# A transposition and a state product of the RWKV pairs issued in turn, on all four quarters of the array

## The chip, the cores and the metric

The kernel runs on one core of a Trainium2 chip. The metric is the device time of one execution in microseconds; of the kernel before there are three runs. A core has five engines that run side by side and wait for one another through semaphores: TensorE (PE in the profile; its weight loads are listed apart as PEld), VectorE (DVE), ScalarE (ACT), GpSimd (POOL), and SyncE (SP), which here issues most DMAs. Products land in PSUM, which ScalarE and VectorE empty.

TensorE is an array of 128 rows by 128 columns. A product whose two sizes are at most 64 needs only one quarter of it. Which quarter is settled by where the operands and the result lie: the rows by the partitions of the operands (0 to 63, or 64 to 127), the columns by the partitions of the result.

## The reference

A decoder trunk of two layers over 1024 tokens of width 1024, in float32. The first layer mixes with 8 retention heads and 8 RWKV-7 heads of width 64, the second with sliding-window attention; each layer has a SwiGLU block. The RWKV heads carry a state that every token updates:

```python
def step(state, inp):
    r_t, w_t, k_t, v_t, a_t, b_t = inp
    sa = jnp.einsum('bhij,bhj->bhi', state, a_t)
    state = state * w_t[:, :, None, :] + sa[..., None] * b_t[:, :, None, :] + v_t[..., None] * k_t[:, :, None, :]
    return state, jnp.einsum('bhij,bhj->bhi', state, r_t)
```

The kernel does this in chunks of 64 tokens. For each chunk it forms the products of the keys and decays among themselves, inverts a triangular matrix for the effect of each token on the later ones (the solve), and then steps the state once a chunk.

## The kernel before, in words

The first mixer (`mixer0`, L502) works on two halves of 512 tokens. Its work is written as Python generators, each with a letter: `a` the first norm; `b` to `e` the four units (two pairs of heads each: a half's pairs 0 and 1, or 2 and 3); `f` to `m` the eight pairs of RWKV heads (`pair`); `n` to `u` the eight retention heads' pairs (`ret`); `v` the second half's norm. `F` is the input projection, `W` the first half's output projection. The class `Plan` (L156) runs these generators against a virtual clock (`plan.now`) of estimated PE time and an account of PSUM banks in use (`plan.banks`), and so settles the order in which the program is emitted. The order of the products on PE is then fixed by hand: `PE_ORDER` (L105) lists entries such as `f11:16`, the next 16 products into the 12th PSUM tile (counted from 0) of stream f, or `f5,6:8`, eight products in turn from tiles 5 and 6. `pe_order` (L312) chains them. The orders on the other engines and the DMA queues are left to the framework, which schedules with a simulated timeline.

A pair works on two heads at once, head 0 in partitions 0 to 63 and head 1 in 64 to 127, over 8 chunks. The tiles of PSUM that matter here are all of the tag "m", of which there are four buffers (banks) for all streams together; `pst` (L390) hands them out in turn, and the next tile of a buffer waits until the one before has been read. A pair's tiles, in order: 0 and 1 the low-rank projections, 2 the norm, 3 the triangular matrix (DT) for the solve, 4 the bonus (bv, L869), 5 to 8 the matrices GG (read by VectorE, L885), 9 and 10 the transposition of BK (L891), and then:

- tile 11 (L894 to L899): the transposition of AR, as 16 products with the identity, head 0 on rows and columns 0 to 63, head 1 on rows and columns 64 to 127: the two diagonal quarters of the array. ScalarE copies the result to the first half of the tile XA.
- tiles 12 and 13: transpositions of v by 128 columns (L304), from which VectorE makes UV (L908 to L928).
- tile 14 (L934 to L939): 16 products of GG by UV. Here head 0's result comes from operands in partitions 64 to 127 and head 1's from 0 to 63: the other two quarters. ScalarE copies the result to the second half of XA.

The unit of the pair reads XA only after its solve (31 steps on VectorE, L966 and L970, a trip through DRAM, and products into tiles of tag "c"), for the products of GT by XA. In `PE_ORDER` tile 11 stands before the transpositions of v and tile 14 some microseconds later, with products of other streams between them. The retention stream emits into the same four banks: tiles 0 and 1 transposed k and v (L1174, L1176), 2 and 3 the scores (masked by VectorE, L1191), 4 the chunk states (L1213), 5 and 6 the outputs (6 is ps_m<-r,Sc), 7 the norm. `second_norm` (L663) loads the second half of x and squares it on ScalarE (L673); later its gained copies (L578, L579) become the second half's operand of F.

Of the kernel before, what the change touches and what calls it, by code (L numbers as in the profile page):

```python
# [10 lines left out]
F32 = mybir.dt.float32  # L11
# [5 lines left out]
P = 128  # L17
# [8 lines left out]
NCH = 8  # L26
# [77 lines left out]

PE_ORDER = """  # L105
F0:13 F1:2 F0:3 F1:14 F0:3 F1:3 F0:3 F1:3 F0:2 F1:2 F2:2 a0:1 F2:22 F3:24 f0:1 f1:1 F4:24 F5:24 F6:15 f2:1 F6:9
F7:24 g0:1 g1:1 F8:9 f3:16 F8:9 g2:1 F8:6 F9:18 f4:1 F9:6 F10:6 f5,6:8 f7,8:8 F10:17 f9:8 f10:8 f11:16 f12:4
g3:16 f13:4 n0:4 n1:4 g4:1 F10:1 F11:12 f14:16 g5:1 g6:2 g5:2 g6,5:3 g7:1 g8:2 g7:2 F11:12 F12:3 g8,7:3 g9:8
g10:8 F12:13 g11:16 g12:4 n2,3:8 g13:4 F12:8 F13:5 n4:8 n5:8 F13:16 n6:8 g14:16 F13:3 F14:21 n7:1 F14:3 F15:24
F16:6 o0:4 o1:4 F16:18 F17:3 o2,3:8 o4:8 F17:21 o5:1 o6:1 o5:7 b0:32 o6:7 h0:1 h1:1 F18:18 b1:32 o7:1 F18:6  # L110
F19:12 b2:8 h2:1 b3:8 b4:8 F19:12 b5:8 b6:16 b7:8 b8:8 F20:24 F21:13 b9:16 b10:8 h3:16 b11:8 b12:4 F21:8 i0:1
i1:1 b13:4 F21:3 F22:24 F23:6 b14:4 i2:1 F23:6 b20:1 b15:4 b20:15 b21:6 b16:4 b21:4 b22:16 b23:5 F23:9 b23:1
b21:2 b17:4 b23:6 h4:1 F23:3 F24:11 b21:1 b18:4 b21:1 b23:2 h5:4 b21:1 b19:4 b21:1 b23:2 F24:12 h6:4 b24:1 F24:1
F25:24 F26:7 b25:1 b26:1 h7:4 h8:4 b27:1 h9:8 F26:11 h10:8 h11:16 h12:4 i3:16 h13:4 p0:4 F26:6 F27:9 p1:4 i4:1
p2:2 p3:2 p2,3:4 h14:16 i5,6:4 i5:2 i6:2 i7:4 i8:4 F27:15 F28:2 p4:8 i9:8 i10:8 F28:6 i11:16 i12:4 p5:8 p6:8
i13:4 F28:16 F29:19 v0:1 p7:1 i14:16 F29:5 F30:7 q0:4 q1:4 F30:3 F31:2 F30:3 F31:11 q2,3:8 F30:9 F31:6 F30:2
F31:2 q4:8 q5:8 F31:3 F32:6 q6:8 F32:18 F33:22 q7:1 c0:32 F33:2 F34:23 c1:32 F34:1 F35:20 c2:8 c3:8 c4:8 j0:1
F35:4 F36:11 j1:1 c5:8 c6:16 c7:8 c8:8 j2:1 F36:9 c9:16 c10:8 c11:8 c12:2 F36:4 F37:10 c12:2 F37:14 F38:7 j3:5
c13:4 j3:11 k0:1 k1:1 F38:8 c20:5 c14:4 c20:11 c21:6 c22:1 c21:2 c15:4 c22:15 c23:4 c21:2 c23:1 c16:4 c23:5 k2:1
F38:9 F39:8 c17:4 c21:2 c23:2 j4:1 F39:16 F40:2 c21:1 c18:4 c21:1 c23:2 j5:4 c21:1 c19:4 c21:1 c23:2 F40:3 j6:4  # L120
F40:19 F41:12 c24:1 F41:12 F42:24 c25:1 c26:1 j7,8:8 c27:1 j9:8 F43:13 j10:8 j11:16 j12:4 k3:16 j13:4 k4:1
F43:11 F44:11 j14:16 k5,6:8 k7:4 k8:4 F44:9 k9:8 k10:8 k11:16 k12:4 r0:4 r1:4 F44:4 F45:10 k13:4 r2,3:8 r4:8
F45:12 k14:16 r5:8 r6:8 l0:1 l1:1 F45:2 F46:17 r7:1 l2:1 F46:7 F47:24 m0:1 m1:1 F48:24 F49:1 l3:1 F49:17 d0:1
l3:3 d0:31 l3:12 m2:1 d1:32 F49:6 F50:15 d2:8 d3,4:16 d5:8 F50:9 F51:2 d6:16 d7:8 m3:16 d8:8 d9:16 d10:8 d11:8
F51:8 s0,1:8 d12:4 F51:14 F52:2 d13:4 F52:19 s2:1 d14:4 s3,2:7 F52:3 F53:3 d15:4 s4:8 F53:18 s5:2 d16:4 s6:8
d20:3 s5:6 d17:4 d20:13 d21:13 d18:4 d21:1 d22:16 d23:3 d21:1 d19:4 d21:1 d23:13 l4:1 F53:3 F54:14 m4:1 s7:1
l5:3 l6:3 l5:1 l6:1 d24:1 F54:10 F55:17 d25:1 d26:1 F55:7 F56:9 l7:4 l8:4 d27:1 l9:8 l10:8 l11:16 l12:4 m5:3
m6:3 m5:1 m6:1 l13:4 F56:15 m7:2 m8:2 m7,8:4 m9:8 m10:8 t0:4 t1:4 F57:24 m11:16 m12:4 t2:4 e0:2 t3:4 l14:16
m13:4 t4:8 t5:8 t6:4 e0:4 m14:1 t6:4 m14:15 e0:26 F58:24 F59:15 t7:1 e1:32 u0:4 u1:4 F59:9 W0:7 e2:8 e3:8 e4:8
u2:4 W0:17 W1:11 u3:4 e5:8 u4:8 e6:16 e7:8 e8:8 u5:8 u6:8 e9:16 e10:8 e11:8 e12:2 u7:1 e20:5 e12:2 e20:11 e21:4  # L130
e22:6 e13:4 e22:10 e23:4 e21:2 e14:4 e23:2 W1:13 W2:14 e15:4 e21:1 W2:10 W3:13 e21:1 e23:2 e21:1 e16:4 e21:1
e23:2 W3:11 W4:9 e17:4 e21:2 e23:2 W4:15 W5:4 e21:1 e18:4 e21:1 e23:2 W5:20 e19:4 e21:2 W6:24 W7:3 e23:2 e24:1
e25:1 e26:1 e27:1 W7:21
"""


# [121 lines left out]
class Kern:  # L258
# [518 lines left out]
    def pair(self, u, hf, p):  # L777


        nc, mp = self.nc, self.mp  # L780
        V, S, G = nc.vector, nc.scalar, nc.gpsimd
        ident = self.cst["ident"]
        half = (slice(0, 64), slice(64, 128))
# [8 lines left out]
        ps = self.pst("m", [P, HT])  # L792
# [15 lines left out]
        ps = self.pst("m", [P, HT])  # L808
# [14 lines left out]
        AR = self.t(mp, [P, NCH, P], "AR", 4)  # L823
# [12 lines left out]
        ps = self.pst("m", [P, NCH, 64])  # L836
# [13 lines left out]
        for q in range(4):  # L850
            r0 = 32 * q
# [14 lines left out]
        ps = self.pst("m", [P, HT])  # L866
# [8 lines left out]
        for h in range(2):  # L875
            pss = [self.pst("m", [P, 4, P]) for _ in range(2)]
            for i in range(4):
                for e in range(2):
                    c = 4 * h + i
# [7 lines left out]
        for e in range(2):  # L887
            ps = self.pst("m", [P, NCH, 64])
            rs = half[e]
# [1 line left out]
                self.tr(ps[:, c, :], BK[rs, c, e : e + 2, :].rearrange("p a t -> p (a t)"), ident[rs, rs])  # L891
            S.copy(GG[:, :, e, P:], ps)
        yield (), 0.6
        XA = self.t(mp, [P, NCH, P], "XA", 2)  # L894
        ps = self.pst("m", [P, NCH, 64])
        for c in range(NCH):
            for rs in half:
                self.mm(ps[rs, c, :], AR[rs, c, 0:64], ident[rs, rs], start=True, stop=True)
        S.copy(XA[:, :, 0:64], ps)  # L899
        UV = self.t(mp, [P, NCH, 2, 64], "UV", 2)  # L900
        UVw = UV.rearrange("p (j two) e t -> p j two e t", two=2)
        for w in range(2):
            ps = self.pst("m", [P, 4, 2, 64])
# [27 lines left out]
                )  # L931
            yield (), 1.0
        yield (), 7.5
        ps = self.pst("m", [P, NCH, 64])  # L934
        for c in range(NCH):
            for e in range(2):
                b = half[1 - e]
                self.mm(ps[half[e], c, :], GG[b, c, e, 0:64], UV[b, c, e, :], start=True, stop=True)
        S.copy(XA[:, :, 64:P], ps)  # L939
        st.update(AR=AR, UV=UV, bv=bv, PC=PC, GG=GG, XA=XA)  # L940
        self.plan.done(f"a{u}_{p}")

    def unit(self, u, hf, pairs):
# [77 lines left out]
        for st, GT in zip(sts, GTs):  # L1021
            GG, XA, UV = st["GG"], st["XA"], st["UV"]
            for h in range(2):
                cc = slice(4 * h, 4 * h + 4)
                ps = self.pst("m", [P, 4, P])
                for i in range(4):
                    for a in half:
                        self.mm(ps[a, i, :], GT[a, 4 * h + i, :], XA[a, 4 * h + i, :], start=True, stop=True)
                for e, a in enumerate(half):
# [5 lines left out]
        for st in sts:  # L1035
            GG, XA, UV, AR = st["GG"], st["XA"], st["UV"], st["AR"]
            M, C0 = XA[:, :, 0:64], XA[:, :, 64:P]
# [1010 lines left out]
```

## Time and profile before

| | |
|---|---|
| median of three runs | 2292.93 us (2292.22 to 2293.02) |
| the profiled execution's own time | 2295.7 us |
| its span, first to last instruction | 2293.9 us |
| PE busy | 2261.0 us, 99% of the span, 13056 instructions |
| DVE, ACT, POOL busy | 74%, 46%, 44% |
| granted TensorE clock, mean | 0.997 |
| first mixer | about the first 660 us |

A row of the view in order of time gives the start in microseconds from the span's start, the length from the first start to the last end, the engine, the line, the operation, output tile and inputs, the shape, and how many instructions were merged; in brackets the idle time of the engine before it and who ended it. A row "64*64" used 64 rows and 64 columns of the array. A float32 product is two instructions (passes) on PE, so 16 products show as x32. The view of waits gives who waited for whom, the sum in microseconds, how often, and the longest. The view of one line or tile gives shortest, median and longest duration in ns, and first and last start.

### The profile page before, as it was taken

What the parts mean: (1) busy time and instruction counts of PE and PEld (TensorE: products, weight loads), DVE (VectorE), ACT (ScalarE), POOL (GpSimd) and SP (SyncE); (2) the same over time, 40 slices, a digit from 0 to 9 for tenths busy, and PEclk for the clock granted to TensorE, in tenths of its full rate; (3) what the DMA queues carried; (4) which work ended last, traced back from release to release, by engine and by line L of the source; (5) the groups of instructions that cost most, each with busy time, mean ns of one, the idle gap of its engine ahead of it and who ended that gap; (6) DMA issues with size and microseconds to landing.
All of it is one profiled execution on the core that took longest, in us unless ns stands there. A gap on an engine that the chain in (4) does not pass through costs nothing.

```text
span 2293.9 us, 35742 instructions
## 1 busy us (share of the span) xinstructions
PE 2261.0 (99%) x13056; PEld 1810.2 (79%) x13056; DVE 1698.6 (74%) x2635; ACT 1047.1 (46%) x1947; POOL 1006.5 (44%) x796
## 2 busy tenths in 40 slices
PE   8999999999999999999999999999999999999998
PEld 6777777778878888888888887787788888888886
DVE  6877855876567358888896967858748788888867
ACT  5454544424445333333343466656745333333335
POOL 3123221202341067777777501113203677778675
PEclk9999999999999999999999999999999999999999
DMA  7566644444446455556766332123246566557663
GB/s 271 194 214 207 195 150 136 140 116 125 144 182 219 164 179 211 211 202 220 261 224 245 108 120 71 52 92 124 85 140 226 171 215 215 210 202 279 226 225 115
DMA packets 170337, 406.43 MB, mean 177 GB/s; under 512 B 43185, under 2 KB 45873, under 8 KB 170161
## 3 DMA queue, kind: packets, MB, share of 16 engines
q1 hardware_dynamic: 166752, 397.59, 50.5%
q10 hardware_dynamic: 2832, 4.45, 0.5%
q8 instruction: 104, 1.70, 0.3%
q0 software_dynamic: 576, 2.10, 0.2%
q14 instruction: 73, 0.59, 0.1%
HBM read 275.48 MB, written 123.21 MB: 174 GB/s over the span
## 4 chain that ended last, share of the span: by engine, by line
PE 77%; DVE 10%; ACT 5%; DMA 3%; issue 3%; SPq 1%; POOL 1%; DVEq 0%; ACTq 0%; POOLq 0%
PE ps_f L293 9%; PE ps_m L1300 7%; PE ps_m L1303 7%; PE ps_m L1302 7%; PE ps_m L293 6%; PE ps_f L1300 5%; PE ps_f L1302 5%; PE ps_f L1303 5%; PE ps_f L450 2%; PE ps_f L447 2%; PE ps_f L449 2%; PE ps_r L1300 2%; PE ps_c L1303 2%; PE ps_r L1303 2%; PE ps_r L1302 2%
## 5 line engine op out<-in xcount | busy, mean ns | idle before, releaser
L293 PE MATMUL ps_f<-n,w 128*128 128x512 f32 x1440 | 360.8, 404 | 9.7 <-ACT w L432 5.8
L293 PEld LDWEIGHTS ps_f<-n,w 128*128 128x128 f32 x1440 | 268.4, 190 | 84.4 <-issue 14.1
L433 POOL TENSOR_TENSOR w<-wr,w 128x512 fp32r<-128x512 f32 x63 | 87.2, 1390 | 300.9 <-ACT w L432 293.3
L432 ACT CAST w<-wr 128x512 fp32r<-128x512 f32 x231 | 141.1, 617 | 160.2 <-PE ps_f L450 53.0
L433 DVE TENSOR_TENSOR w<-wr,w 128x512 fp32r<-128x512 f32 x168 | 117.6, 703 | 64.0 <-ACT w L432 63.5
L1300 PE MATMUL ps_f<-n,w 128*128 128x512 f32 x415 | 164.2, 396 | 0.0
L1302 PE MATMUL ps_f<-n,w 128*128 128x512 f32 x415 | 162.7, 392 | 0.0
L1303 PE MATMUL ps_f<-n,w 128*128 128x512 f32 x415 | 162.6, 392 | 0.0
L433 POOL TENSOR_TENSOR w<-wq,w 128x512 fp32r<-128x512 f32 x91 | 130.5, 1444 | 31.6 <-ACT w L432 31.6
L1300 PE MATMUL ps_m<-n,w 128*128 128x512 f32 x333 | 130.4, 392 | 0.0
L1302 PE MATMUL ps_m<-n,w 128*128 128x512 f32 x333 | 129.6, 389 | 0.0
L1303 PE MATMUL ps_m<-n,w 128*128 128x512 f32 x333 | 129.5, 389 | 0.0
L1310 DVE TENSOR_TENSOR nq<-ps_m,u 128x512 f32<-128x512 f32 x88 | 58.9, 684 | 92.2 <-PE ps_m L1303 92.2
L1730 POOL TENSOR_SCALAR s<-s,st 128x256 f32<-128x256 f32 (+1 forms) x32 | 30.6, 955 | 192.0 <-ACT w L432 61.3
L464 POOL TENSOR_TENSOR n<-nq,n 128x512 fp32r<-128x512 f32 x60 | 100.1, 1681 | 7.6 <-ACT n L462 7.6
L1495 POOL TENSOR_TENSOR w<-wd,w 128x512 fp32r<-128x512 f32 (+1 forms) x62 | 87.8, 1425 | 32.4 <-ACT w L1494 30.5
L1300 PEld LDWEIGHTS ps_f<-n,w 128*128 128x128 f32 x415 | 77.9, 188 | 20.2 <-issue 3.8
L1300 PE MATMUL ps_m<-cb,w 128*128 128x512 f32 x236 | 91.9, 389 | 0.4 <-DVE nq L1310 0.4
L1302 PEld LDWEIGHTS ps_f<-n,w 128*128 128x128 f32 x415 | 77.9, 188 | 17.7 <-issue 2.0
L1303 PE MATMUL ps_m<-cb,w 128*128 128x512 f32 x236 | 91.8, 389 | 0.0
L1302 PE MATMUL ps_m<-cb,w 128*128 128x512 f32 x236 | 91.8, 389 | 0.0
L1303 PEld LDWEIGHTS ps_f<-n,w 128*128 128x128 f32 x415 | 77.9, 188 | 16.8 <-issue 0.7
(521 smaller groups left out, 6494.1 us busy)
## 6 DMA issues: line engine op xcount, KB each, us to landing
hc<-n SPq DMA_DIRECT2D x84, 512.0 KB, 3.2
wsp<-w SPq DMA_DIRECT2D x54, 512.0 KB, 3.3
w<-wsp SPq DMA_DIRECT2D x54, 512.0 KB, 3.5
n<-hc SPq DMA_DIRECT2D x54, 512.0 KB, 6.2
wq<-in_w_gate SPq DMA_DIRECT2D x44, 512.0 KB, 4.5
u<-u SPq DMA_DIRECT2D x88, 256.0 KB, 2.9
ha<-hc SPq DMA_DIRECT2D x34, 512.0 KB, 5.6
hid<-n SPq DMA_DIRECT2D x66, 256.0 KB, 2.0
```

What stands on the lines that cost most here:

```text
L293: i = self.nc.tensor.matmul(out, lhsT, rhs, **kw)
L432: nc.scalar.copy(hi[:, :n], raw[:, c])
L433: self.lo.tensor_tensor(out=lo[:, :n], in0=raw[:, c], in1=hi.bitcast(F32)[:, :n], op=ALU.subtract)
L447: x = nc.tensor.matmul(ps, hi, rh, start=k == 0, stop=False)
L449: y = nc.tensor.matmul(ps, hi, rl, start=False, stop=False)
L450: z = nc.tensor.matmul(ps, lo, rh, start=False, stop=k == n - 1)
L464: e.tensor_tensor(out=lo, in0=src, in1=hi.bitcast(F32), op=ALU.subtract)
L1300: i = mm(ps, hi, xh, start=first and k == 0, stop=False, skip_group_check=True)
L1302: mm(ps, hi, xl, start=False, stop=False, skip_group_check=True)
L1303: mm(ps, lo, xh, start=False, stop=last and k == len(w) - 1, skip_group_check=True)
L1310: self.last_add = V.tensor_tensor(out=o, in0=x, in1=y, op=ALU.add)
L1495: nc.gpsimd.tensor_tensor(out=lo, in0=v, in1=hi.bitcast(F32), op=ALU.subtract)
```

## The change

Tile 11 goes from its place. Its 16 products are issued where those of tile 14 were, one of each in turn, so that successive products use the quarters (rows 0, columns 0), (rows 64, columns 0), (rows 64, columns 64), (rows 0, columns 64), and so on. The two copies to XA follow one another. The transpositions of v are now tiles 11 and 12, and the two groups are tiles 13 and 14, allocated one after the other. The planner's clock and its account of banks are advanced at the old place as if tile 11 were still there and put back at the new one, so that the emission order of all the rest is as before. In `PE_ORDER` each pair's 16 entries of tile 11 are taken out, and the 16 of tile 14 become 32 of both in turn at the same place; nothing else in it moves.

```diff
-        XA = self.t(mp, [P, NCH, P], "XA", 2)
-        ps = self.pst("m", [P, NCH, 64])
-        for c in range(NCH):
-            for rs in half:
-                self.mm(ps[rs, c, :], AR[rs, c, 0:64], ident[rs, rs], start=True, stop=True)
-        S.copy(XA[:, :, 0:64], ps)
+        self.plan.banks.append(self.plan.now + 3.0)
+        for _ in range(2 * NCH):
+            self.plan.now += max(0.05, 0.00167 * 64 * 0.6)
...
         yield (), 7.5
-        ps = self.pst("m", [P, NCH, 64])
+        XA = self.t(mp, [P, NCH, P], "XA", 2)
+        pa, ps = (self.pst("m", [P, NCH, 64]) for _ in range(2))
+        self.plan.banks.pop()
+        now = self.plan.now
+        for c in range(NCH):
+            for e in range(2):
+                b = half[1 - e]
+                self.mm(pa[half[e], c, :], AR[half[e], c, 0:64], ident[half[e], half[e]], start=True, stop=True)
+        self.plan.now = now
         for c in range(NCH):
             for e in range(2):
                 b = half[1 - e]
                 self.mm(ps[half[e], c, :], GG[b, c, e, 0:64], UV[b, c, e, :], start=True, stop=True)
+        S.copy(XA[:, :, 0:64], pa)
         S.copy(XA[:, :, 64:P], ps)
```

The entries of `PE_ORDER` for pair g, before and after; the other seven change in the same way:

```diff
-g10:8 F12:13 g11:16 g12:4 n2,3:8 g13:4 F12:8 F13:5 n4:8 n5:8 F13:16 n6:8 g14:16 F13:3
+g10:8 F12:13 g11:4 n2,3:8 g12:4 F12:8 F13:5 n4:8 n5:8 F13:16 n6:8 g13,14:32 F13:3
```

More of the change, by code (lines that the diff above doesn't have):

```diff
@@ L106 @@
 F0:13 F1:2 F0:3 F1:14 F0:3 F1:3 F0:3 F1:3 F0:2 F1:2 F2:2 a0:1 F2:22 F3:24 f0:1 f1:1 F4:24 F5:24 F6:15 f2:1 F6:9
[L107 to L130, printed above, removed]
@@ L131 @@
-e22:6 e13:4 e22:10 e23:4 e21:2 e14:4 e23:2 W1:13 W2:14 e15:4 e21:1 W2:10 W3:13 e21:1 e23:2 e21:1 e16:4 e21:1
-e23:2 W3:11 W4:9 e17:4 e21:2 e23:2 W4:15 W5:4 e21:1 e18:4 e21:1 e23:2 W5:20 e19:4 e21:2 W6:24 W7:3 e23:2 e24:1
-e25:1 e26:1 e27:1 W7:21
+F7:24 g0:1 g1:1 F8:9 f3:16 F8:9 g2:1 F8:6 F9:18 f4:1 F9:6 F10:6 f5,6:8 f7,8:8 F10:17 f9:8 f10:8 f11:4 g3:16
+f12:4 n0:4 n1:4 g4:1 F10:1 F11:12 f13,14:32 g5:1 g6:2 g5:2 g6,5:3 g7:1 g8:2 g7:2 F11:12 F12:3 g8,7:3 g9:8 g10:8
+F12:13 g11:4 n2,3:8 g12:4 F12:8 F13:5 n4:8 n5:8 F13:16 n6:8 g13,14:32 F13:3 F14:21 n7:1 F14:3 F15:24 F16:6 o0:4
@@ new lines @@
+o1:4 F16:18 F17:3 o2,3:8 o4:8 F17:21 o5:1 o6:1 o5:7 b0:32 o6:7 h0:1 h1:1 F18:18 b1:32 o7:1 F18:6 F19:12 b2:8
+h2:1 b3:8 b4:8 F19:12 b5:8 b6:16 b7:8 b8:8 F20:24 F21:13 b9:16 b10:8 h3:16 b11:8 b12:4 F21:8 i0:1 i1:1 b13:4
+F21:3 F22:24 F23:6 b14:4 i2:1 F23:6 b20:1 b15:4 b20:15 b21:6 b16:4 b21:4 b22:16 b23:5 F23:9 b23:1 b21:2 b17:4
+b23:6 h4:1 F23:3 F24:11 b21:1 b18:4 b21:1 b23:2 h5:4 b21:1 b19:4 b21:1 b23:2 F24:12 h6:4 b24:1 F24:1 F25:24
+F26:7 b25:1 b26:1 h7:4 h8:4 b27:1 h9:8 F26:11 h10:8 h11:4 i3:16 h12:4 p0:4 F26:6 F27:9 p1:4 i4:1 p2:2 p3:2
@@ new lines @@
+p2,3:4 h13,14:32 i5,6:4 i5:2 i6:2 i7:4 i8:4 F27:15 F28:2 p4:8 i9:8 i10:8 F28:6 i11:4 p5:8 p6:8 i12:4 F28:16
+F29:19 v0:1 p7:1 i13,14:32 F29:5 F30:7 q0:4 q1:4 F30:3 F31:2 F30:3 F31:11 q2,3:8 F30:9 F31:6 F30:2 F31:2 q4:8
+q5:8 F31:3 F32:6 q6:8 F32:18 F33:22 q7:1 c0:32 F33:2 F34:23 c1:32 F34:1 F35:20 c2:8 c3:8 c4:8 j0:1 F35:4 F36:11
+j1:1 c5:8 c6:16 c7:8 c8:8 j2:1 F36:9 c9:16 c10:8 c11:8 c12:2 F36:4 F37:10 c12:2 F37:14 F38:7 j3:5 c13:4 j3:11
+k0:1 k1:1 F38:8 c20:5 c14:4 c20:11 c21:6 c22:1 c21:2 c15:4 c22:15 c23:4 c21:2 c23:1 c16:4 c23:5 k2:1 F38:9 F39:8
@@ new lines @@
+c17:4 c21:2 c23:2 j4:1 F39:16 F40:2 c21:1 c18:4 c21:1 c23:2 j5:4 c21:1 c19:4 c21:1 c23:2 F40:3 j6:4 F40:19
+F41:12 c24:1 F41:12 F42:24 c25:1 c26:1 j7,8:8 c27:1 j9:8 F43:13 j10:8 j11:4 k3:16 j12:4 k4:1 F43:11 F44:11
+j13,14:32 k5,6:8 k7:4 k8:4 F44:9 k9:8 k10:8 k11:4 r0:4 r1:4 F44:4 F45:10 k12:4 r2,3:8 r4:8 F45:12 k13,14:32 r5:8
+r6:8 l0:1 l1:1 F45:2 F46:17 r7:1 l2:1 F46:7 F47:24 m0:1 m1:1 F48:24 F49:1 l3:1 F49:17 d0:1 l3:3 d0:31 l3:12 m2:1
+d1:32 F49:6 F50:15 d2:8 d3,4:16 d5:8 F50:9 F51:2 d6:16 d7:8 m3:16 d8:8 d9:16 d10:8 d11:8 F51:8 s0,1:8 d12:4
@@ new lines @@
+F51:14 F52:2 d13:4 F52:19 s2:1 d14:4 s3,2:7 F52:3 F53:3 d15:4 s4:8 F53:18 s5:2 d16:4 s6:8 d20:3 s5:6 d17:4
+d20:13 d21:13 d18:4 d21:1 d22:16 d23:3 d21:1 d19:4 d21:1 d23:13 l4:1 F53:3 F54:14 m4:1 s7:1 l5:3 l6:3 l5:1 l6:1
+d24:1 F54:10 F55:17 d25:1 d26:1 F55:7 F56:9 l7:4 l8:4 d27:1 l9:8 l10:8 l11:4 m5:3 m6:3 m5:1 m6:1 l12:4 F56:15
+m7:2 m8:2 m7,8:4 m9:8 m10:8 t0:4 t1:4 F57:24 m11:4 t2:4 e0:2 t3:4 l13,14:32 m12:4 t4:8 t5:8 t6:4 e0:4 t6:4
+m13,14:32 e0:26 F58:24 F59:15 t7:1 e1:32 u0:4 u1:4 F59:9 W0:7 e2:8 e3:8 e4:8 u2:4 W0:17 W1:11 u3:4 e5:8 u4:8
@@ L134 @@
+e6:16 e7:8 e8:8 u5:8 u6:8 e9:16 e10:8 e11:8 e12:2 u7:1 e20:5 e12:2 e20:11 e21:4 e22:6 e13:4 e22:10 e23:4 e21:2
+e14:4 e23:2 W1:13 W2:14 e15:4 e21:1 W2:10 W3:13 e21:1 e23:2 e21:1 e16:4 e21:1 e23:2 W3:11 W4:9 e17:4 e21:2 e23:2
+W4:15 W5:4 e21:1 e18:4 e21:1 e23:2 W5:20 e19:4 e21:2 W6:24 W7:3 e23:2 e24:1 e25:1 e26:1 e27:1 W7:21
 """
```

## The prediction

> **What bounds the kernel now.** I read the first page first, then the table by stretches, then the waits of PE, and last the order of time around the two products that the change touches.
>
> ```profile
> span 2293.9 us, 35742 instructions
> PE   8999999999999999999999999999999999999998
> ```
>
> PE is busy nine tenths or more in every slice but the ends, so a product removed from PE is worth its own length, if PE finds its next product ready. How often it doesn't is in the stretches. Columns: length, then busy time and instructions of PE, PEld, DVE, ACT, POOL, then clock, DMA share, GB/s.
>
> ```profile
> 96.30:121.00 24.70, 23.36 (x215) 18.69 (x211) 23.50 (x72) 9.06 (x14) 1.29 (x1) 1.00 0.44 163
> 240.40:284.50 44.10, 39.37 (x341) 30.77 (x339) 42.47 (x94) 25.48 (x39) 12.72 (x9) 0.99 0.63 199
> 291.00:407.00 116.00, 116.00 (x1085) 89.77 (x1080) 63.46 (x125) 50.55 (x73) 23.57 (x41) 1.00 0.46 141
> 407.20:455.60 48.40, 47.12 (x410) 36.21 (x408) 43.68 (x110) 20.51 (x32) 13.66 (x20) 1.00 0.46 145
> 530.00:660.00 130.00, 130.00 (x1235) 104.66 (x1234) 75.26 (x134) 60.08 (x105) 39.57 (x30) 1.00 0.40 138
> 0.00:660.00 660.00, 640.80 (x5651) 500.42 (x5652) 462.48 (x962) 299.43 (x487) 161.10 (x195) 0.99 0.53 172
> ```
>
> The mixer is the first 660 us; PE idles 19.2 us of it. In two stretches PE never idles (291 to 407, 530 to 660): there the gain passes whole. In three others VectorE is nearly full (23.50 of 24.70, 42.47 of 44.10, 43.68 of 48.40): there a quicker PE may only wait longer. Those waits:
>
> ```profile
> PE ps_f L293 <- ACT w L432: 5.8, 1, 5.8
> PE ps_f L293 <- DVE n L579: 3.3, 1, 3.3
> ...
> PE ps_m L293 <- DVE r L1176: 1.7, 2, 1.1
> ...
> PE ps_m L293 <- ACT XA L939: 1.6, 1, 1.6
> ...
> PE ps_m L293 <- DVE UV L915: 0.6, 1, 0.6
> ```
>
> Of the copies that the change moves, one (L939) is awaited today, for 1.6 us.
>
> **The change part by part.** Per pair, of eight (streams f to m), 16 products that transpose AR (tile 11) leave their place and come in turn with the 16 of GG by UV (old tile 14). Each float32 product is two passes, so both groups show as x32. Pair f:
>
> ```profile
> 80.86 1.15 PE L293 MATMUL ps_m<-c_ident,AR 64*64 64x64 f32 x32
> 81.94 0.66 PE L304 MATMUL ps_m<-c_ident,rv 128*128 128x128 f32 x4
> ...
> 89.02 1.15 PE L293 MATMUL ps_m<-UV,GG 64*64 64x64 f32 x32
> 90.10 1.83 PE L293 MATMUL ps_m<-AR,BK 64*128 64x128 f32 x26
> ```
>
> From start to next start each group takes 1.08 us. One pass lasts:
>
> ```profile
> L293 PE MATMUL ps_m<-c_ident,AR x256: 218/218/268, 80.9 to 549.7; 64*64 64x64 f32 x128
> ```
>
> 1.15 less the last pass's 0.22 leaves 0.93 for 16 rounds of two passes: 58 ns a round, two quarters at work, and 0.15 until the next kind of product starts. Tile 11 uses the two diagonal quarters of the array, tile 14 the other two.
>
> Do four quarters run at once? The trace has it once, in pair g, where the last products of a retention head (diagonal quarters) meet the UV group:
>
> ```profile
> 113.69 0.76 PE L293 MATMUL ps_m<-r,Sc 64*64 64x128 f32 x10
> 114.19 0.27 PE L293 MATMUL ps_m<-UV,GG 64*64 64x64 f32 x2
> 114.29 0.28 PE L293 MATMUL ps_m<-r,Sc 64*64 64x128 f32 x2
> 114.30 0.28 PE L293 MATMUL ps_m<-UV,GG 64*64 64x64 f32 x4
> ...
> 114.54 0.81 PE L293 MATMUL ps_m<-UV,GG 64*64 64x64 f32 x22
> 115.27 0.97 PE L293 MATMUL ps_f<-n,w 128*128 128x512 f32 x3
> ...
> 425.63 1.09 PE L293 MATMUL ps_m<-r,Sc 64*64 64x128 f32 x16
> 426.65 0.70 PE L293 MATMUL ps_m<-wa,wua 64*128 64x512 f32 x2
> ```
>
> Alone the r,Sc group takes 1.02 (425.63 to 426.65) and the UV group 1.08, together 2.10; here both took 1.58 (113.69 to 115.27), and the UV group's 1.08 did not stretch. Two quarters in one bank, two in another: the change's pattern. So I take 16 rounds of 58 ns with four passes each, two more starts 10 ns apart (114.29, 114.30): 1.10 us in place of 2.16, **1.06 us a pair**. Bounds: 2 x 0.93 + 0.15 = 2.01 if quarters take turns (0.15 a pair left), 1.06 if they don't.
>
> The Trainium skill's "TensorE: Matmul & The Clock Gate", Part 3, says that a weight load overlaps products in flight only where the row group differs. In the new order every second neighbour shares its rows (quarter 3 follows 2, 1 follows 4), where today none does; by the rule half the overlap would go, and with it the gain. The trace speaks against it: the groups that alternate columns on the same 128 rows keep the same 1.08:
>
> ```profile
> 179.49 1.15 PE L293 MATMUL ps_m<-UV,GG 128*64 128x64 f32 x32
> 180.57 1.09 PE L293 MATMUL ps_m<-GG 64*64 64x128 f32 x16
> ```
>
> In pairs g and m the new group stands behind r,Sc products on the diagonal, where the UV group hid before. In g: r,Sc 0.87 (1.02 less 0.15), then 0.93 + 0.15, is 1.95 against 1.58: 0.37 back. For m, with half as many r,Sc products beside it but its bank awaiting VectorE's last Sc, I take the same, 0.35.
>
> **Banks and copies.** No DMA, and no work of VectorE, is added or moved. ScalarE's copy of the transposition only moves:
>
> ```profile
> L899 ACT COPY XA<-ps_m x8: 586/586/597, 82.1 to 550.0; 128x512 f32<-128x512 f32 x8
> ```
>
> 0.59 us each, on an engine that is busy 299.43 of 660 us; it now stands directly before the copy of GG UV, and nothing reads XA before its unit's solve is through, so by itself it costs nothing. But four banks serve all "m" tiles in turn. Without old tile 11 everything from there to tile 14 shifts by one bank, and in place of one bank two are taken at once: the GG UV bank is the one of the third tile before, the next two tiles get those of the second and the first before, and the third and fourth wait for the two copies. PE's order is written by hand, so behind a waiting product stands all of PE. In most pairs those tiles are long emptied. In two they aren't:
>
> ```profile
> 242.19 1.15 PE L293 MATMUL ps_m<-UV,GG 64*64 64x64 f32 x32
> 243.27 2.17 PE L293 MATMUL ps_m<-AR,BK 64*128 64x128 f32 x24
> 246.99 1.16 PE L293 MATMUL ps_m<-AR,BK 64*128 64x128 f32 x8 [1.55 <-ACT XA L939]
> ...
> 245.83 0.63 ACT L673 ACTIVATE nq<-nq 128x512 f32<-128x512 f32 x1 [1.49 <-DMA nq<-in_xT]
> 246.37 0.57 ACT L939 COPY XA<-ps_m 128x512 f32<-128x512 f32 x1
> ...
> 423.30 1.15 PE L293 MATMUL ps_m<-UV,GG 64*64 64x64 f32 x32 [0.31 <-DVE UV L928]
> ...
> 423.07 0.68 DVE L1191 TENSOR_TENSOR r<-ps_m,c_dmask 128x512 f32<-128x512 f32 x1
> ```
>
> Pair h: PE waits 1.55 for the copy, which stands behind an activation that waits for a DMA. Now the second copy stands behind the first: 0.57 later. A wait for the bonus tile's bank just before falls inside those 1.55. Pair k: the UV group starts at 423.30; its bank is that of the first masked scores, read until 423.75: 0.45.
>
> Now the waits that swallow a lead. I carry PE's lead through the mixer; a wait on work that PE itself released earlier keeps it, one on a full VectorE cuts it to the lead that VectorE had on entering the stretch.
>
> ```profile
> 107.26 0.69 PE L293 MATMUL ps_m<-r,r 128*64 128x64 f32 x16 [0.59 <-DVE UV L915]
> ...
> 419.36 0.69 PE L293 MATMUL ps_m<-r,r 128*64 128x64 f32 x16 [0.53 <-DVE r L1176]
> ...
> 284.58 1.65 PE L293 MATMUL ps_f<-n,w 128*128 128x512 f32 x3 [3.25 <-DVE n L579]
> ```
>
> - f (81): lead 1.06. g's transposition (100) lies in the first full stretch; its 1.08 is lost at 107.26. Less 0.37: 0.69.
> - h (233): 1.77, less 0.57 at the copy. i (255): PE gains 1.06 more, but at 284.58 VectorE decides, which entered with 1.77: 1.77.
> - j (395): 2.83. k (411): its 1.08 is lost at 419.36; less 0.45: 2.38.
> - l (533): 3.44. m (549): 1.08 less 0.35: 4.17. PE has no idle time from 530 to 660, so this reaches the rest, where 1620.2 of 1633.9 us are PE's.
>
> Sum: **4.2 us**, from 2295.7 (span 2293.9) to 2291.5 in the profiled execution. The median of the runs is 2.8 lower, 2292.93; carried there: **2288.7**. About 0.2% (4.6 us) is what a measurement of this kernel can tell from no change, so the forecast lies at that edge. The planner keeps its clock, but the order of VectorE, ScalarE and the queues is settled by the framework and may shift; the trace can't show that. The 13 us of idle PE after the first load (19.2 less 5.8) bound what it could give; as much it could cost; I take nothing, and 2 us to each side.
>
> **The rivals.**
> 1. All passes: VectorE's order adapts, or its leads are larger than I carry. 8 x 1.06 less 0.37 and 0.35: 7.8, 2285.1. For it: two stretches without a wait. Against: the 107.26, 284.58 and 419.36 rows.
> 2. The quarters take turns: 8 x 0.15 = 1.2 less the cuts at h and k: about 2292.5. Against it stands 1.58 in place of 2.10. The row-group rule of the Trainium skill ("TensorE: Matmul & The Clock Gate", Part 3) would bring this out.
> 3. Slower: the copies. A pair now needs two before the banks turn. If the framework puts them behind a waiting activation as in h today (1.55) in six pairs, PE loses 9.3, and 9.3 less 4.2 is 5.1: 2298.0. Break-even is 0.5 us a pair (4.2/8); from 1.1 a pair it is slower by over 0.2%. Against: one of eight copies is awaited today. "TensorEngine Tiling (Array Packing)" of the Trainium skill, PSUM Bottleneck, warns that tiling speeds the products and not the emptying; the 1.55 agrees.
> 4. The clock. Around the 3.25 wait it halves:
>
> ```profile
> 283.94:290.77 6.83, 6.19 (x19) 4.47 (x21) 6.63 (x17) 0.00 (x0) 0.38 (x3) 0.50 0.53 160
> ```
>
> 6.83 us at 0.50 cost 3.4. A shifted wait may miss it (2285.3) or, longer elsewhere, bring a second (2292.1).
>
> **How the numbers follow.** Forecast 0.50, its own range 2286.5 to 2291, half of it below the edge (2288.3); all passes 0.17; turns 0.12; slower 0.14; clock 0.07 (0.04 gain). Faster: 0.23 + 0.17 + 0.04 = 0.44; same: 0.27 + 0.12 + 0.03 = 0.42; slower 0.14. The range 2284.5 to 2295 leaves out the slower rival and the last of the others.
>
> **What would show it.** A mixed group of 64 passes that takes about 1.10 us, with starts of both tiles within 10 ns; if it takes 2.0, rival 2 holds. The v transpositions 1.08 earlier. Longer waits at the rows of 107, 284 and 419. In h, a wait on the second copy. A wait on either copy in other pairs, or XA copies far behind their products, would make the prediction wrong; so would a second row at 0.50.

## The result, and the profile after

Over 16 runs of each the changed kernel takes 2296.77 us (median; 2295.45 to 2298.77), the kernel before 2292.84 (2290.77 to 2295.41). The ratio is 1.0016, 95% interval 1.0009 to 1.0022: 3.9 us slower, where 4.2 us faster was forecast. The profiled execution took 2297.24, span 2295.4. Line numbers of the new kernel are one lower up to the pair's tile 11 and five higher behind the pair. One entry of `PE_ORDER` differs from the description: in pair m the first of the old 16 products stood ahead of four products of the retention stream, and now all 32 stand behind them.

The first page, the stretches and the waits of PE within the mixer, columns as before:

```profile
span 2295.4 us, 35736 instructions
PE 2257.8 (98%) x13056; PEld 1806.0 (79%) x13056; DVE 1699.0 (74%) x2635; ACT 1047.3 (46%) x1947; POOL 1009.6 (44%) x796
```

```profile
240.40:284.50 44.10, 40.43 (x320) 31.66 (x310) 42.64 (x103) 24.65 (x39) 11.19 (x8) 0.92 0.51 166
291.00:407.00 116.00, 113.28 (x1045) 86.79 (x1045) 63.17 (x119) 49.14 (x71) 22.83 (x38) 0.99 0.45 140
407.20:455.60 48.40, 45.32 (x320) 34.87 (x317) 43.26 (x110) 17.85 (x28) 12.67 (x20) 0.96 0.44 132
0.00:660.00 660.00, 636.15 (x5644) 495.02 (x5645) 465.31 (x960) 297.81 (x484) 162.30 (x194) 0.99 0.52 171
```

```profile
PE ps_m L303 <- DVE GG L884: 3.6, 3, 2.5
PE ps_m L292 <- ACT XA L943: 2.9, 1, 2.9
PE ps_m L292 <- DVE Sc L1218: 2.6, 2, 2.2
```

Over the whole span PE is less busy than before (2257.8 against 2261.0 us), although more of its work ran at half clock: the products did get shorter. But it idles for 23.9 us of the first 660 instead of 19.2, also in a stretch that had no idle time (113.28 busy of 116.00). After the first load, the old profile had one wait of 3.25 us and none other above 1.55; now three are over 2 us.

**The products do what the change says.** Pair f in order of time:

```profile
87.60 0.27 PE L292 MATMUL ps_m<-c_ident,AR 64*64 64x64 f32 x1
87.61 0.27 PE L292 MATMUL ps_m<-UV,GG 64*64 64x64 f32 x1
87.61 0.27 PE L292 MATMUL ps_m<-c_ident,AR 64*64 64x64 f32 x1
87.62 0.27 PE L292 MATMUL ps_m<-UV,GG 64*64 64x64 f32 x1
...
88.55 0.22 PE L292 MATMUL ps_m<-UV,GG 64*64 64x64 f32 x1
88.69 1.97 PE L292 MATMUL ps_m<-AR,BK 64*128 64x128 f32 x26
```

Four starts within 20 ns, 64 passes in 1.09 us (87.60 to 88.69); 1.10 was forecast.

**The clock.** In each profile, from the first products to the end of the layers, the stretches at half clock are 3.41 or 6.83 us long and lie on one grid with a step of 3.41 us; a step is called a frame here. The same view as the stretches, for three frames with a long wait in them and for what follows each:

```profile
240.66:244.07 3.41, 1.24 (x19) 1.04 (x16) 3.24 (x9) 1.28 (x3) 1.26 (x1) 1.00 0.85 305
244.07:250.90 6.83, 6.10 (x23) 5.28 (x24) 6.49 (x20) 1.78 (x4) 1.27 (x1) 0.50 0.05 15
291.86:295.27 3.41, 1.16 (x12) 0.58 (x12) 2.82 (x8) 0.50 (x1) 0.19 (x1) 1.00 0.67 107
295.27:298.68 3.41, 3.41 (x12) 2.64 (x9) 2.91 (x6) 1.19 (x3) 1.36 (x3) 0.50 0.64 253
411.32:414.74 3.42, 1.12 (x16) 1.10 (x16) 3.22 (x11) 0.38 (x1) 0.00 (x0) 1.00 0.18 72
414.74:418.15 3.41, 3.41 (x17) 3.10 (x16) 3.17 (x12) 1.63 (x4) 0.00 (x0) 0.50 0.00 0
```

Where PE was busy for 1.1 to 1.2 of 3.41 us, the next 3.41 or 6.83 us ran at 0.50: 13.65 us here, worth 6.8, against 6.83 us (3.4) in the old profile. The runs say the same: the granted clock over the whole span averages 0.9959 in the 16 runs of the new kernel, 0.9977 to 0.9981 in the runs of the old one beside the experiments. Of some 2295 us that is 9.3 us lost against 4.4 to 5.3, a difference of 4.0 to 4.9: as much as the 3.9 that the kernel got slower. This is an estimate, and an upper one, as a slower clock costs only where PE is what the rest waits for. Nor is the clock the whole account: run e15 below has the clock of run e1 within 0.0003 and is 0.0018 slower.

**Where the long waits come from.** The largest, on VectorE:

```profile
287.51 0.68 DVE L754 TENSOR_TENSOR z<-ps_f,rs 128x512 f32<-128x512 f32 x1
292.36 0.90 DVE L998 STREAM_TRANSPOSE TZ<-GT 32x256 f32<-32x256 f32 x2 [4.17 <-DMA GT<-dg]
293.29 0.28 DVE L1218 SCALAR_TENSOR_TENSOR Sc<-Sc,c_gam,ps_m 128x64 f32<-128x64 f32 x1
293.48 0.42 DVE L998 STREAM_TRANSPOSE TZ<-GT 32x256 f32<-32x256 f32 x1
293.84 0.23 DVE L1218 SCALAR_TENSOR_TENSOR Sc<-Sc,c_gam,ps_m 128x64 f32<-128x64 f32 x1
```

VectorE stands 4.17 us at a transpose whose input is still on its way from DRAM, and behind it in the queue stand the Sc updates for which PE waits. In the old kernel these updates ran at 291.3 to 292.5, between steps of the solve, well ahead of the products that read them (294.35), and the transposes came later:

```profile
291.30 0.28 DVE L1213 SCALAR_TENSOR_TENSOR Sc<-Sc,c_gam,ps_m 128x64 f32<-128x64 f32 x1 [0.56 <-PE ps_m L293]
```

The second place is on ScalarE, in pair h:

```profile
241.88 0.63 ACT L672 ACTIVATE nq<-nq 128x512 f32<-128x512 f32 x1 [1.00 <-DMA nq<-in_xT]
243.64 0.63 ACT L672 ACTIVATE nq<-nq 128x512 f32<-128x512 f32 x1 [1.13 <-DMA nq<-in_xT]
244.18 0.57 ACT L943 COPY XA<-ps_m 128x512 f32<-128x512 f32 x1
244.65 0.59 ACT L944 COPY XA<-ps_m 128x512 f32<-128x512 f32 x1
```

Both copies stand behind two squares that wait for loads; before, the copy stood behind one. The third place is in pair k. SyncE issued a weight load ahead of the load of the solve's matrix, VectorE waited longer for that matrix (before, then after), and PE waited 2.45 us for VectorE's GG products:

```profile
407.15 0.19 DVE L966 TENSOR_TENSOR xt<-X,DT 128x31 f32<-128x31 f32 x1 [2.09 <-DMA DT<-dn]
```

```profile
410.52 0.19 DVE L971 TENSOR_TENSOR xt<-X,DT 128x31 f32<-128x31 f32 x1 [4.64 <-DMA DT<-dn]
```

Except for the copies, none of these instructions is in the diff. VectorE, GpSimd and SyncE are given the same instructions in the same order of emission in both kernels, but the queues came out different: through the first mixer in 224 of 720 places on VectorE, 13 of 170 on GpSimd, 38 of 285 on SyncE, and 14 of 395 on ScalarE (with a pair's two copies side by side in both). The likely reason is that the framework schedules by a simulated timeline, in which the products now end at other times; no run shows that step itself.

### The profile page after: what moved, and what is told of

Read it like the earlier page. It is cut to its first block, busy times and chain, and to the rows that moved or that the text cites. A ratio compares the mean times of both kernels' runs of the same rounds, so it can differ in the third digit from the quotient of the medians.

```text
span 2295.4 us, 35736 instructions
## 1 busy us (share of the span) xinstructions
PE 2257.8 (98%) x13056; PEld 1806.0 (79%) x13056; DVE 1699.0 (74%) x2635; ACT 1047.3 (46%) x1947; POOL 1009.6 (44%) x796
## 4 chain that ended last, share of the span: by engine, by line
PE 78%; DVE 10%; ACT 4%; DMA 3%; issue 2%; SPq 1%; POOL 1%; DVEq 0%; ACTq 0%; POOLq 0%
PE ps_f L292 10%; PE ps_m L1305 8%; PE ps_m L1307 7%; PE ps_m L1308 7%; PE ps_f L1305 5%; PE ps_f L1307 5%; PE ps_f L1308 5%; PE ps_m L292 5%; PE ps_f L449 2%; PE ps_f L446 2%; PE ps_f L448 2%; PE ps_r L1305 2%; PE ps_r L1308 2%; PE ps_r L1307 2%; PE ps_c L1305 2%
```

## The experiments

Theory 1: the mixed groups gain what was forecast, and the new order of the other engines' queues costs more than that. Theory 2: the two banks and two copies at once cost it, whatever the order. To tell them apart, a helper (`pin_queues`) chains the instructions of the four engines through the first mixer in a given order (dependencies without semaphores, as `pe_order` does for PE):

```diff
         self.pe_order()
+        self.pin_queues()
...
+        for e, text in QUEUES.items():
+            mine = [x for x in ins if x.engine == eng[e]]
...
+                        self.tc.add_manual_dep(
+                            x, last.name,
+                            mybir.DependencyInfo(mybir.DependencyClass.NoSync, mybir.DependencyReason.DATA), reason="order",
```

`QUEUES` lists an order as numbers in emission order: "old" is that of the kernel before, "new" that of the changed kernel. Each ratio is to runs of the kernel before beside it, whose median was 2292.30 to 2294.38 us from call to call, so that ratios compare better than times; the clock is the mean of the runs. A difference of two ratios is uncertain by about 0.0011 to 0.0014, some 2.5 to 3 us. No run repeats a kernel's own orders with the helper and nothing else; e10 (the changed kernel, new orders) and e8 (the kernel before, old orders), with one small edit each, came out at 1.0015 and 0.9996, so nothing points to a cost of the helper itself.

| run | what | median us | ratio (95%) | clock |
|---|---|---|---|---|
| changed kernel | new orders | 2296.77 | 1.0016 (1.0009 to 1.0022) | 0.9959 |
| e1 | change, old orders | 2289.08 | 0.9983 (0.9974 to 0.9992) | 0.9980 |
| e2 | old products, new orders | 2301.04 | 1.0029 (1.0018 to 1.0040) | 0.9962 |
| e3 | e1, groups not in turn | 2289.87 | 0.9989 (0.9981 to 0.9997) | 0.9981 |
| e4 | the kernel before | 2292.20 (one run) | | 0.999 |
| e5 | e1, h's copies first | 2288.92 | 0.9973 (0.9962 to 0.9983) | 0.9978 |
| e6 | e1, new order in h and i | 2298.48 | 1.0014 (1.0006 to 1.0023) | 0.9966 |
| e7 | e1, new order in k | 2289.50 | 0.9980 (0.9971 to 0.9989) | 0.9976 |
| e8 | old kernel, h's copy first | 2293.66 | 0.9996 (0.9987 to 1.0005) | 0.9980 |
| e9 | new orders, Sc before TZ | 2292.88 | 0.9997 (0.9988 to 1.0006) | 0.9966 |
| e10 | new orders, h's copies first | 2297.24 | 1.0015 (1.0006 to 1.0024) | 0.9960 |
| e11 | e9 and e10 | 2292.69 | 0.9997 (0.9988 to 1.0006) | 0.9971 |
| e12 | e5, groups not in turn | 2291.26 | 0.9986 (0.9977 to 0.9995) | 0.9982 |
| e13 | e11, Sc near 254 first too | 2292.97 | 0.9999 (0.9990 to 1.0007) | 0.9971 |
| e14 | e13 without h's copies first | 2296.79 | 1.0016 (1.0007 to 1.0025) | 0.9963 |
| e15 | e11, old order in k | 2293.42 | 1.0001 (0.9992 to 1.0010) | 0.9977 |
| e16 | e11, old order in f and g | 2294.30 | 1.0006 (0.9997 to 1.0015) | 0.9975 |

**e1 and e2: the order alone.**

> The changed kernel with VectorE, ScalarE, GpSimd and SyncE held to the order in which the kernel before issued the first mixer's work (each pair's AR copy stands directly before its GG UV copy; everything else in the old order). Theory 1 (the loss is the order that the framework chose anew on the other engines): the time falls to about 2288.7 us, which is 2292.8 less the 4.2 of the prediction, and the three waits of PE that the changed kernel has and the old one not (2.90 at the copies of pair h, 2.23 at Sc, 2.45 at GG of pair k) shrink to about 2.1, 0 and under 0.5. Theory 2 (two banks taken at once, with two copies, cost it, whatever the order): the waits stay and the time is 2295 us or more. In between, each part has its share.

> The kernel before, with the same four engines held to the order in which the changed kernel issued its work; the AR copy of each pair, which stands elsewhere there, is left free. Theory 1 (order): the old products pay the new order's waits without the gain of the mixed groups: 2292.8 plus 3.9 plus 4.2, about 2301 us, with a wait of over 2 us near 290 at Sc and near 410 at GG. Theory 2 (banks): the order alone costs nothing, 2292.8 us within 1 us.

Both came out as theory 1 had them: 2289.08 (2288.7 expected) and 2301.04 (2301). By the ratios the order costs the changed kernel 0.0033 of the time, 7.6 us, and the old one 0.0029, 6.6 us. Theory 2 falls. The clock (0.9980 in e1 against 0.9959) accounts for at most some 4.8 of the 7.6 us; the rest is the waits themselves. The waits of PE between 230 and 300 us, in e1 and then in e2:

```profile
PE ps_f L347 <- DVE n L652: 2.2, 2, 1.2
PE ps_m L347 <- ACT XA L1017: 2.0, 1, 2.0
```

```profile
PE ps_m L348 <- DVE Sc L1287: 2.6, 2, 2.2
PE ps_m L348 <- ACT XA L1013: 2.1, 1, 2.1
```

With the old orders the Sc wait is gone; with the new ones it is there without the change too.

**e4: the kernel before, again.**

> The kernel before, once more, for a second profile. If the wait of 3.25 us near 284.6 and the halved clock behind it belong to the kernel, both come again at the same place, and the span is 2293.9 within 1 us. If they were an accident of the one profiled execution, they are gone and the span is about 2290.5, 3.4 us less.

The span was 2290.4, and the wait of 3.25 with its halved clock was gone (two of 1.20 and 1.07 in its place). Its time was 2292.20, beside a median of 2292.30. So they do not come in every execution, and the prediction was built on one that had them. Nor are they an accident of that one: of the 129 runs of the kernel before beside the experiments, 24 had a granted clock of 0.999 like e4, and 31 one of 0.997 like the first profile; and e8's profile, of the old kernel with one edit, has a wait of 3.17 us there and the halved clock behind it.

**e6 and e7: which stretch.** `QUEUES` is old outside the stretch and new in it.

> The changed kernel in the old orders, save the stretch of pairs h and i (about 235 to 300 us), where VectorE, ScalarE, GpSimd and SyncE have the order of the changed kernel. Theory 1: it takes back what that stretch lost there: a wait of about 2.2 us at Sc and about 0.9 us more at the copies of h, each with half of 3.4 us or more of halved clock: 2289.1 plus 4 to 5, about 2293.5 us. If these waits were accidents of one profile: 2289 us.

> The changed kernel in the old orders, save the stretch of pair k (about 400 to 430 us), where VectorE, GpSimd and SyncE have the order of the changed kernel; SyncE then issues a weight load ahead of the load of the solve's matrix. Theory 1: the solve's matrix lands about 3 us later, VectorE's GG products stand behind the first steps of the solve, PE waits about 2.4 us for them and the clock halves for 3.4 us: 2289.1 plus 2.4 plus 1.7, less the wait of 1.2 at 416 that this hides: about 2292 us. If the place of that load doesn't matter: 2289 us.

The stretch of h and i holds the loss, all of it within the uncertainty: 1.0014 less 0.9983 is 0.0031, 7.1 us of 7.6, where 4 to 5 were expected. That of k holds none (0.9980); there theory 1 was wrong about the third wait, which in e7's profile was 1.59 us, was followed by no halved clock, and took the place of one at 416. The waits of e6, 230 to 300 us:

```profile
PE ps_m L347 <- DVE Sc L1292: 2.7, 3, 2.1
PE ps_m L347 <- ACT XA L1017: 2.6, 1, 2.6
```

**e9, e10 and e11: which place in it.** In the new orders, the only edits are these two:

```diff
 VectorE, near 293 us
-TZ TZ Sc TZ Sc wa Sc TZ z Sret
+Sc Sc wa Sc z TZ TZ TZ TZ Sret
 ScalarE, pair h
-nq nq XA(AR) XA(GG UV)
+XA(AR) XA(GG UV) nq nq
```

> The changed kernel with all engines held to its own new orders, and one edit: on VectorE the four transposes TZ of GT, which wait for a load from DRAM (4.17 us in the changed kernel), stand behind the four Sc updates and two evacuations that they stood ahead of. Theory 1a (that one place is the larger half of the loss): PE's waits of 2.2 and 0.4 us near 293 and the halved clock behind them (3.41 us at 0.50, worth 1.7) go, 4.3 of the 7.1 us that the stretch of h and i costs: about 0.9973 to 0.999 times... in us, 2296.8 less 4.3, 2292.5, about the time of the kernel before. Theory 1b (the copies of pair h are the whole loss): 2296.8.

> The changed kernel in its own new orders, and one edit on ScalarE: the two copies of pair h stand ahead of both squares that wait for loads. Theory 1a: PE's wait there (2.90 us) and the halved clock behind it (6.83 us at 0.50, worth 3.4) go, but VectorE's waits at 281 to 287 take part of it back, as in the run with the old orders, where this edit was worth 0.2 to 2 us: 2296.8 less 1 to 3, about 2294.8 us. Theory 1b (the copies of pair h are the whole loss): 2289 to 2290 us.

> The changed kernel in its own new orders with both edits: the Sc updates ahead of the transposes TZ, and the copies of pair h ahead of the squares. If these two places are the loss and nothing else in the new order is: the time of the run with the old orders or of that with the copies of h first, 0.9973 to 0.9983 of the kernel before, 2287 to 2289 us. If the rest of the new order (the solve of i done ahead of the gained copies, the queues of SyncE) costs as well: 2290 to 2293 us.

Here the fourth update (Sret) stays where it was; three Sc updates and two evacuations pass the four transposes (TZ). That gives 4.4 us (1.0016 to 0.9997; 4.3 expected), or 4.1 between e10 and e11, which differ in this edit alone. So theory 1a holds for this place. The copies give nothing, alone or with it, against an expected 1 to 3, and theory 1b falls. For the copies the reason lies in another queue. PE and then VectorE in e11:

```profile
251.36 0.44 PE L347 MATMUL ps_m<-r,Sc 64*64 64x128 f32 x4
254.30 1.23 PE L347 MATMUL ps_m<-r,Sc 64*64 64x128 f32 x12 [2.50 <-DVE Sc L1292]
```

```profile
253.16 0.69 DVE L505 TENSOR_TENSOR w<-wr,w 128x512 fp32r<-128x512 f32 x1
253.76 0.29 DVE L1045 TENSOR_TENSOR xt<-X,DT 128x136 f32<-128x136 f32 x1
253.97 0.27 DVE L1292 SCALAR_TENSOR_TENSOR Sc<-Sc,c_gam,ps_m 128x64 f32<-128x64 f32 x1
```

PE no longer waits for the copies; it waits 2.50 for other Sc updates, which VectorE, busy for 44.71 of the 46 us from 240 to 286, does behind steps of the solve.

**e13 and e14: that place as well.** The four updates near 254 (three Sc and Sret) are moved directly behind the last GG product, with the copies of h first (e13) and late (e14).

> The changed kernel in its own new orders with three edits: the copies of pair h ahead of the squares, the Sc updates near 293 ahead of the transposes TZ, and, new, the four Sc updates near 254 directly behind the last GG product instead of behind twelve more steps of the solve and two low parts of weights. With the first two edits PE waited 2.50 us for those Sc and the clock halved behind it (3.41 us at 0.50). If the new order costs by such blockings of VectorE in three places and nothing else: that wait goes, and the time falls from 0.9997 of the kernel before to that of the old orders, 0.9973 to 0.9983 (2.5 plus 1.7 less what the waits at 274 to 284 take back: 2 to 4 us). If something else in the new order costs the rest: 0.999 to 0.9997.

> The same without the edit on ScalarE: the two Sc places mended, the copies of pair h behind both squares as in the changed kernel. If VectorE's order is the whole loss and the copies only shift a wait that comes anyway: the same time as with three edits, within 1 us. If the copies cost once nothing hides them: PE waits 2.3 us at the copies and the clock halves, 2 to 4 us longer than with three edits.

The wait at 254 went in e13, and 1.79 and 2.61 us at n (L651) came; e13 (0.9999) is no faster than e11 (0.9997), where the first reading had expected 2 to 4 us less. VectorE is full, so a wait moved is not a wait less. e14 lost 3.8 us to e13, for a reason that its VectorE shows:

```profile
254.20 0.28 DVE L1291 SCALAR_TENSOR_TENSOR Sc<-Sc,c_gam,ps_m 128x64 f32<-128x64 f32 x1 [3.25 <-PE ps_m L346]
```

PE waited 3.1 us for the late copies; the Sc updates, now early in the queue, waited for PE; so the engine that sets this stretch stood still for 3.25 us. In e9, with the same late copies, the solve's steps ahead of Sc filled that time.

**e5 and e8: the copies in the old orders.** The ScalarE edit above. In the old orders the copies stand behind one square only, and pass that one.

> The changed kernel in the old orders, and on ScalarE the two copies of pair h stand ahead of the square that waits for a load (in the run with the old orders: square with 1.86 us of waiting, then the two copies, then PE's wait of 2.01 us). Theory 1 (the copies are late because of what they stand behind, not because there are two): PE's wait in pair h goes from 2.0 to under 0.3 us and no halved clock follows it; 2289.1 less 2.0, or less 3.7 where the 3.4 us of halved clock went too: 2285.5 to 2287 us. Theory 2 (the two banks themselves are the limit): a wait of over 1 us stays. Third: the wait goes, but VectorE's waits at 276 and 283 (1.15 and 1.08) grow by what is gained: 2288 to 2289 us.

> The kernel before, in its own orders, with the one copy of pair h ahead of the square that waits for a load. If the order of that copy is worth something with or without the change, PE's wait there (1.55 and 0.92 us in the two profiles of the kernel before) goes and the time falls by 0.5 to 1.5 us, to about 2291.3. If VectorE's waits at 276 and 284 take it back: 2292.3 us.

The waits are those of the third outcome for e5: the wait at the copies went, and one of 2.8 us for n came:

```profile
PE ps_f L347 <- DVE n L652: 2.8, 1, 2.8
```

By the times the outcomes can't be told apart: 0.9973 against e1's 0.9983 and e8's 0.9996 against 1 are within the intervals. e5 has the lowest ratio of all, 0.9973 (0.9962 to 0.9983), clear of the kernel before and of the changed kernel, but not of e1 and e7.

**e3 and e12: not in turn.** One edit, for all eight pairs:

```diff
-f13,14:32
+f13:16 f14:16
```

> As the changed kernel held to the old orders, but the two groups are issued one after the other (the 16 products of AR, then the 16 of GG UV) at the same place and into the same two banks. If the gain is that four quarters run at once, a pair's groups take about 2.16 us from start to start in place of 1.09, PE is busy 8 x 1.07 = 8.6 us longer, and the time is longer than in the run with turns by 4 us (half of it hidden in waits, as the prediction counted) to 8.6 us: about 2293 to 2297 us. If the turns don't matter, the time is that of the run with turns.

> As the run in the old orders with the copies of pair h first (0.9973 of the kernel before), but each pair's two groups one after the other instead of in turn. In the trace a pair's groups then take 1.84 us from start to start in place of 1.09, 6.0 us for eight pairs. If the turns' gain passes where PE is the bound (pairs i, j, l and m at least), the time is 3 to 6 us longer: 0.9986 to 0.9999 of the kernel before. The first run without turns was only 0.0006 longer than its twin; if that holds (waits on VectorE swallow the gain nearly everywhere), 0.9973 to 0.998.

Pair f in e3 (whose one profiled execution, with 2296.26 us, was slower than the median; only the products' own times are read from it, and e12 shows the same 1.84):

```profile
87.07 0.97 PE L347 MATMUL ps_m<-c_ident,AR 64*64 64x64 f32 x26
87.83 0.27 PE L347 MATMUL ps_m<-UV,GG 64*64 64x64 f32 x2
87.88 0.28 PE L347 MATMUL ps_m<-c_ident,AR 64*64 64x64 f32 x3
...
88.00 0.98 PE L347 MATMUL ps_m<-UV,GG 64*64 64x64 f32 x27
88.91 0.83 PE L347 MATMUL ps_m<-AR,BK 64*128 64x128 f32 x10
```

The two groups take 1.84 us from start to start, not 2.16: the first two passes of UV start ahead of the last six of AR, which stand before them in `PE_ORDER` and use the other two quarters. The turns add 0.75 us a pair, 6.0 for eight. Of these 0.0006 and 0.0013 arrived (e3 less e1, e12 less e5), 1.4 and 3.0 us, each uncertain by about 3. So part of the change's gain is had by putting the two groups beside one another (e3 is at 0.9989, 2.5 us below the kernel before), and what the turns themselves add, some 2 us, is not shown to be more than nothing by either run alone.

**e15 and e16: the rest.** The two mends of e11 leave 0.0014 (3 us) to e1 and 0.0024 (5.5 us) to e5.

> The changed kernel in its new orders with two edits (copies of pair h ahead of the squares, Sc near 293 ahead of the transposes TZ), and in addition the stretch of pair k (400 to 430 us) in the old order. With the two edits alone it took 0.9997 of the kernel before; its profile shows at 409 us a wait of 2.41 us for GG of pair k and 3.41 us of halved clock behind it. If those are the rest that is missing to the old orders: 0.9978 to 0.9985. If pair k's order costs nothing, as the run with that stretch alone in the new order had it (0.9980): 0.9997.

> The same two edits, and the stretch of pairs f and g (75 to 235 us) in the old order, that of k in the new. If the missing rest comes from f and g: 0.998 to 0.9985. If VectorE, which is full from 240 to 290 us, ends the advantage of anything ahead of it, the order of f and g changes nothing: 0.9997 within 0.0009.

Neither stretch brings it (1.0001 and 1.0006). By elimination, with e6, it lies in the rest of the new order between 235 and 300 us; no run shows it there, and which place it is stays open.

## Why the prediction was wrong

- **The step that failed** is the one named last in the sum: "the order of VectorE, ScalarE and the queues is settled by the framework and may shift; the trace can't show that ... I take nothing, and 2 us to each side". It was 7.6 us to one side (e1 against the changed kernel), 7.1 of them between 235 and 300 us, 4.4 at one place. The bound on it, 13 us of idle PE, was not passed; the 2 us had no row behind them. Those 13 us also belonged to one execution: the longest wait in them, 3.25, was not there in e4.
- **The rest of the sum** gave 2288.7, and with the old order the change takes 2289.08 (0.9983: 3.9 us gained, between 1.8 and 6.0; 4.2 forecast). That the whole fits so well is in part luck, as the terms below show. The group: 1.09 us for 1.10. Pair g: from the first r,Sc product to the next F product 1.95 us, as forecast:

```profile
111.73 0.97 PE L292 MATMUL ps_m<-r,Sc 64*64 64x128 f32 x13
...
113.68 2.58 PE L292 MATMUL ps_f<-n,w 128*128 128x512 f32 x10
```

- **Copies and banks.** Pair h waits 2.01 us in e1 against 1.55 and 0.92 in the two profiles before; 0.57 more was forecast. But the size of this wait is that of one execution: e7, with the same order there, waits 0.9, because its square waited 0.74 us for its load and not 1.86. The forecast took one such wait for the kernel's.
- **Leads.** PE's lead is read here against e4, which has no halved clock in the mixer. Of the runs with the groups in turn only e7 has none either, and its orders up to pair j are the old ones. Its lead is 1.79 us at the r,Sc products behind pair i (289.03 against 290.82), for 1.77 forecast, and 2.85 at the products of pair j, for 2.83 (e4, then e7):

```profile
401.17 1.15 PE L293 MATMUL ps_m<-UV,GG 64*64 64x64 f32 x32
```

```profile
398.32 0.27 PE L347 MATMUL ps_m<-c_ident,AR 64*64 64x64 f32 x1
```

- In e1 the lead at pair i was gone (291.04): its longer wait in h was followed by 3.41 us at half clock, worth 1.7. The sum has no such term and leaves it to rival 4.
- **Pair k.** Here the lead in the sum was too large. VectorE sets when the products behind the masked r can start (e4, then e1):

```profile
415.77 0.69 PE L293 MATMUL ps_m<-r,r 128*64 128x64 f32 x16 [0.42 <-DVE r L1176]
```

```profile
415.95 0.69 PE L347 MATMUL ps_m<-r,r 128*64 128x64 f32 x16 [1.18 <-DVE r L1255]
```

- So of a lead of 0.86 us at j nothing was left there in e1, and of 1.77 in e5 0.58 was left. The forecast took away only k's own 1.08, so k cost about 1.1 us more. From there to the r,Sc products behind k's group e1 and e5 lose 0.44 and 0.45, for 0.45 forecast. Pairs l and m gave 1.7 in e1 for 1.79 forecast. All these are readings of one execution of each kernel.
- **Rival 1** (7.8 us, all passes): falls; e1's gain ends at 6.0, and VectorE took most of the lead at pair k. **Rival 2** (quarters take turns, 2.0 us a group; its terms add up to 2292.7 rather than 2292.5): falls. Every second neighbour shares its rows with the one before it, and four starts still lie within 20 ns; what the Trainium skill's "TensorE: Matmul & The Clock Gate", Part 3, makes of shared row groups is not seen for these passes.
- **Rival 3** (copies behind waiting activations, 2298.0): near in time by luck, and wrong in place. Its row, the 1.55, was a wait for a load ahead of the copy, and not the copy's own 0.57. The order it feared came about in one pair of eight, and there the copies alone cost nothing while VectorE was behind (e10), 3.8 us once VectorE waited for them (e14 less e13). The engine that should have been named is VectorE, with work for PE queued behind a wait for DRAM.
- **Rival 4** (a second halved clock, 2292.1): it came, at three places in the profile, and the clock's share, 4.0 to 4.9 us by the estimate above, is as large as the whole loss. It was carried as a case of its own, with 0.07, though it follows most waits over 2 us, those of rival 3 too.

## What to carry to other kernels

Where a scheduler with a simulated timeline orders the queues, a shorter instruction changes orders far from it; compare the engines' orders of the two programs first, and hold the old ones to see what the edit itself is worth. In a queue, look for an instruction that waits for DRAM ahead of one that the busiest engine waits for: here four such transposes cost 4.4 us, about what eight pairs of products gained (3.9). In a stretch that another engine fills, a mend moves the wait, and one that makes that engine stand lengthens the time.

## What the runs showed of the hardware

- The halved clock needs no frame without work. It comes in frames of 3.41 us. In the 18 profiles there are, after the first products and up to the end of the layers, 24 frames with PE busy for 0.75 to 1.62 us, and all 24 were followed by 3.41 or 6.83 us at 0.50; of the 43 frames with 1.65 to 2.3 us busy, five were. So where a wait lies on the grid counts as well as its length: of the 29 waits of 2.0 us or more, the twelve of 2.45 and more were all followed by a halved clock, and thirteen of the seventeen shorter ones. The longest single wait in the changed kernel's frame at 291.86 was 2.23 us. The Trainium skill ("TensorE: Matmul & The Clock Gate", Why this matters for your kernels) allows gaps of about 3 us before the clock drops; here a wait of 2.2 was enough, and the measurement decides.
- Products for free quarters of the array overtake: in e3 the first UV pass starts at 87.83, and the last AR pass, which stands before it in `PE_ORDER`, at 88.00. In the old kernel's pair g, UV passes (from 114.19) start among the last r,Sc passes in the same way.
